# Four sums of weights per unit of a Strassen down projection: two by accumulating transfers from GpSimd's queue, two on VectorE

## The chip, the cores and the metric

The kernel runs on one core of a Trainium2 chip. A core has a matrix engine (TensorE, PE in the profile), a vector engine (VectorE, DVE), a scalar engine (ScalarE, ACT), a general engine (GpSimd, POOL) and a sync engine (SyncE, SP), each with its own instruction queue. Transfers between main memory and the core's on-chip memory are issued from these queues and carried out by 16 DMA engines. The metric is the time of one execution in microseconds, the median of several runs.

## What is computed

The kernel is one inference step of one encoder layer for 1024 prompt frames and 128 sample frames, in float32:

```python
def swiglu(x, w_gate, w_up, w_down):
    return (jax.nn.silu(x @ w_gate) * (x @ w_up)) @ w_down
...
        x = x + 0.5 * swiglu(rms_norm(x, norm_ffn1[l]), w_ffn1_gate[l], w_ffn1_up[l], w_ffn1_down[l])
        m, s_new, conv_new, pool_new = mixer(rms_norm(x, norm_mix[l]), w_in[l], conv_w[l], a_log[l],
        ...
        x = x + m
        x = x + 0.5 * swiglu(rms_norm(x, norm_ffn2[l]), w_ffn2_gate[l], w_ffn2_up[l], w_ffn2_down[l])
```

The model is 1024 wide, the hidden layer of the SwiGLU 2816. The mixer (gated DeltaNet and multi-scale pooling) is not touched here. The change lies in the last product of each SwiGLU, `@ w_down`, which runs twice per execution.

## The kernel before

**Float32 from three products.** A matrix is split into a high part (rounded by a cast) and a low part (what is left), and each product of weights W and operand H is formed as high x high + high x low + low x high. Every block of weights therefore goes through `piece` (L275): ACT casts it into the high half of a tile of the ring O (L287), DVE subtracts to get the low half (L288). PE's matmuls all stand on one line, L58.

**Chunks and units.** The 1152 tokens are three chunks: chunk 0 of 512, chunks 1 and 2 of 320 each. The down projection of chunk 0 (`down0`) is a plain product. Chunks 1 and 2 go together through `down12`, a Strassen-Winograd scheme: the weights are cut into 2 x 2 blocks a11, a12, a21, a22 and seven products of sums of blocks replace eight. One *unit* (g, d) of `down12` makes the seven products for one column block d of the output (d = 0 to 3) and one group g of hidden blocks. The groups have 4, 3 and 4 blocks of 128, so a unit has 84 matmuls in groups 0 and 2 (weight tiles of 128 x 512), and 63 in group 1 (128 x 384). There are 12 units per stage and two stages, 24 units in all.

**The sums.** Three products take a block as it is (a11, a12, a22), four take sums, all formed by POOL before the change:

- T1 takes a21 + a22 (L282),
- T2 takes `sm` = a21 + a22 + a11 (L286, in the same call of `piece`),
- B22 takes `sm` + a12 (L282),
- T3 takes a11 + a21 (L282).

The buffers of the sums are "s" and "sum", two of each, in region Q for groups 0 and 1, and in A5 for group 2.

**Where the blocks come from.** `load` issues two DMAs from SP per unit, one with a11 and a12 (L642), one with a21 and a22 (L643), 512 KB each with four blocks, 384 KB with three. Their targets are a ring of four slots (R0, R1, O5, O6), so that a load waits until the blocks of the unit two before are used up. Right after the second load SP issues up to 10 pending loads of operands of the next group (`pace`, g_keep to the A and B regions).

**Order.** A scheduler fixes each engine's order; on each engine it is followed strictly. PE's order in a steady unit u is B11(u), B21(u), T4(u-1), T2(u), B22(u), T1(u+1), T3(u). T1 and B22 accumulate in PSUM tile c, B11, T2, T3 and T4 in tile a, B21 in tile b; between two accumulations DVE adds the state of the tile into x (`add`, L654), and the next product on that tile waits for it. T1 of the next unit is formed ahead, inside the present unit (`fifth`).

Of the kernel before, what the change touches and what calls it, by code (L numbers as in the profile page):

```python
# [10 lines left out]
ALU = mybir.AluOpType  # L11
AX = mybir.AxisListType

P = 128
# [12 lines left out]
GROUPS = [(0, 4), (4, 3), (7, 4)]  # L27
# [13 lines left out]
def trunk(ctx: ExitStack, tc: tile.TileContext, xin, s0, convst, poolst, cm_in, vec_in, small_in,  # L41
# [3 lines left out]
    V, A, G, T, SY = nc.vector, nc.scalar, nc.gpsimd, nc.tensor, nc.sync  # L45

    class Products:

        t = 0.0
# [22 lines left out]
    def nm(s):  # L72
        uid[0] += 1
        return f"{s}_{uid[0]}"

    def pt(tag, shape=None):
        t = psum.tile([P, 512], F32, tag=tag, name=nm("ps_" + tag))
        return t
# [16 lines left out]
    def region(tag, dt=F32):  # L95
        return main.tile([P, SIZE[tag]], dt, tag=tag, name=nm(tag))
# [17 lines left out]
    def xk(c, k):  # L114
        return X[c][k // 4][:, k % 4, :]

    class Slots:


        def __init__(self):  # L120
            self.mem, self.n = {}, {}
# [28 lines left out]
    def pace(ins, most=1):  # L150

        with tc.issue_after(ins):
            for _ in range(min(most, len(pending))):
                pending.pop(0)()
# [113 lines left out]
    class Blocks:  # L268


        def __init__(self, ring):
            self.gs, self.ring, self.n = Slots(), ring, 0

        def piece(self, *src, more=None):

            m = src[0].shape[-1]
            t = region(self.ring[self.n % len(self.ring)], F32R)
            self.n += 1
            hi, lo = t[:, :m], t[:, 512:512 + m]
            if len(src) == 2:  # L280
                t = self.gs.get("s", m)
                G.tensor_add(t, *src)  # L282
                src = [t]
            src = src[0]
            if more:
                G.tensor_add(more[0], src, more[1])  # L286
            Blocks.high = A.copy(hi, src).ins  # L287
            Blocks.mark = V.tensor_sub(lo, src, hi.bitcast(F32)).ins  # L288
            return [x.rearrange("p (k c) -> p k c", c=P) for x in (hi, lo)]

        def product(self, ps, w, hs, start=True, stop=True):
            (whi, wlo), (hhi, hlo) = w, hs
            for k in range(len(hhi)):
                T.matmul(ps, whi[:, k, :], hhi[k], start=start and k == 0, stop=False, skip_group_check=True)
                T.matmul(ps, whi[:, k, :], hlo[k], start=False, stop=False, skip_group_check=True)
                T.matmul(ps, wlo[:, k, :], hhi[k], start=False, stop=stop and k == len(hhi) - 1, skip_group_check=True)
# [44 lines left out]
    def gate_up(wi, wg, wu, gk, H, RB, cs, ahead, norm, x0=None):  # L341


        bl = Blocks([f"O{i}" for i in range(7)])
        gs, piece, product = bl.gs, bl.piece, bl.product

        def load(f, most=1):
# [55 lines left out]
        def fifth(w):  # L403

            be, sm, c3 = pt("c")[:, :N], gs.get("sum", 512), gs.get("c3", N)
            product(be, piece(w[2], w[3], more=(sm, w[0])), op["T1"])
            A.mul(c3, be, -1.0)
            return c3, sm

        def left_gate(al, g1, g2):  # L410

            p1, ga = gs.get("p1", N), pt("b")[:, :N]
            w1 = piece(g1)
            product(al, w1, op["B11"])
            A.copy(p1, al)
            w2 = piece(g2)
            product(ga, w2, op["B21"])
            V.tensor_add(p1, p1, ga)
            A.activation(p1, p1, AF.Silu)
            return p1, w1, w2  # L420
# [191 lines left out]
    def down12(wd, gk, op0, beside, done):  # L612


        bl = Blocks(["O3", "O4", "O0", "O1", "O2"])
        gs, piece, product = bl.gs, bl.piece, bl.product
        for tag in ("R0", "R1", "O5", "O6"):
            gs.place(region(tag), ("raw", 1024, 1))

        def temps(tag):  # L620
            for t in ("s", "sum"):
                gs.mem.pop(t, None)
            gs.place(region(tag), ("s", 512, 2), ("sum", 512, 2))

        ops = {0: op0}

        def ask(g, tags):

            q, n = GROUPS[g]
            op = ops[g] = {}  # L630
            for j, (name, tag) in enumerate(zip(DOWN, tags)):
                t = region(tag, F32R)
                op[name] = [[t[:, (2 * k + s) * N:(2 * k + s + 1) * N] for k in range(n)] for s in range(2)]
                for k in range(n):
                    pending.append(lambda t=t, j=j, k=k: SY.dma_start(
                        t[:, 2 * k * N:2 * (k + 1) * N].bitcast(F32), gk[2][q - AHEAD // 2 + k][j]))

        def load(g, d, most):
            q, n = GROUPS[g]
            o, m = 2 * q * P, n * P  # L640
            raws = gs.get("raw", 2 * m), gs.get("raw", 2 * m)
            SY.dma_start(raws[0], wd[d][:, o:o + 2 * m])  # L642
            pace(SY.dma_start(raws[1], wd[d + 4][:, o:o + 2 * m]).ins, most)  # L643
            return [r[:, i * m:(i + 1) * m] for r in raws for i in range(2)]

        def fifth(g, d, w):

            be, sm = pt("c")[:, :N], gs.get("sum", w[0].shape[-1])
            product(be, piece(w[2], w[3], more=(sm, w[0])), ops[g]["T1"], True, False)
            add(2, d + 4, be, -0.5)  # L650
            return be, sm

        def add(c, d, ps, by=0.5):
            V.scalar_tensor_tensor(xk(c, d), ps, by, xk(c, d), ALU.mult, ALU.add)  # L654

        def ended(g, c, d):
            if g == len(GROUPS) - 1 and done:
                done(c, d)

        def left_low(g, d, al, a22):  # L660

            product(al, piece(a22), ops[g]["T4"], False)
            add(1, d + 4, al, -0.5)
            ended(g, 1, d + 4)

        temps("Q")
        units = [(g, d) for g in range(len(GROUPS)) for d in range(4)]
        nxt = last = None
        ask(1, ["A5", "A0", "A1", "A2", "A3", "A4", "A6"])
        for u, (g, d) in enumerate(units):  # L670
            if not nxt:
                w = load(g, d, 6)
                nxt = w, fifth(g, d, w)
            (a11, a12, a21, a22), (be, sm) = nxt
            op = ops[g]
            al, ga = pt("a")[:, :N], pt("b")[:, :N]
            product(al, piece(a11), op["B11"])
            add(1, d, al)
            product(ga, piece(a12), op["B21"])
            next(beside, None)  # L680
            if last:
                left_low(*last)
            if u == 4:
                ask(2, [f"B{i}" for i in range(7)])
            product(al, piece(sm), op["T2"], False)
            add(1, d, ga)
            ended(g, 1, d)
            add(2, d, al)
            product(be, piece(sm, a12), op["B22"], False)
            add(2, d, be)  # L690
            ended(g, 2, d)
            next(beside, None)
            if u + 1 < len(units):
                g2, d2 = units[u + 1]
                if g2 == 2 and g == 1:
                    temps("A5")
                w = load(g2, d2, 6 if g2 == 0 else 10)
                if g2 != g:
                    rest()
                nxt = w, fifth(g2, d2, w)  # L700
            product(al, piece(a11, a21), op["T3"], False)
            add(2, d + 4, al, -0.5)
            ended(g, 2, d + 4)
            next(beside, None)
            last = g, d, al, a22
        left_low(*last)
        for _ in beside:
            pass
# [38 lines left out]
    def downs(wd, gk, src, done0=None, after=lambda c: (), done12=None):  # L747
# [33 lines left out]
        down0(wd, [(home, first, 0), (second, ask, 2)], sums(), done0)  # L781
        rest()
        down12(wd, gk, op0, iter(after(0)), done12)

        ends = [iter(after(c)) for c in (2, 1)]
# [23 lines left out]
    def rest():  # L809
        while pending:  # L810
            pending.pop(0)()
# [642 lines left out]
    for n in names:  # L1454
        if n[1] in "dHXr":
            continue
        b, w, h = n[0], n[1], n[2]
# [38 lines left out]
    left = list(urgent)  # L1496
    while left or fill or live or cur:
# [4 lines left out]
        if cur is None and fill and all(i in done for i in after[fill[0]]):  # L1502
            n = fill.pop(0)
            cur = [n, max([done[i] for i in after[n]] + [0]), None]
        cand = sorted([(e[0] > T.t, e[0] if e[0] > T.t else 0, n[0], rank[n[1]], n) for n, e in live.items()])
        if cand and (not cand[0][0] or cur is None or cur[1] > cand[0][1]):
            n = cand[0][-1]
            e = live[n]
        elif cur:
            n, e = cur[0], cur[1:]  # L1510
# [165 lines left out]
```

## Time and profile before

| | |
|---|---|
| median of 3 runs | 2192.55 us (2190.09 to 2193.48) |
| profiled execution | 2195.53 us, span 2193.7 us |
| mean granted clock of PE | 0.992 |
| PE, DVE, ACT, POOL busy | 2132.2, 1526.1, 917.5, 684.9 us |
| moved by DMA | 289.72 MB |
| first stage of `down12` | about 621 to 787 us |
| second stage of `down12` | about 2004 to 2177 us |

The profile is of one execution. "Busy" sums the durations of an engine's instructions. A view of waits lists, by line, how long an engine stood idle and which instruction released it: total, number of times, longest. In a timeline each row has the start, the duration, the engine, line and operation, "out<-in", and in brackets the idle time ahead of it with the releaser. Rows of the chain of waits tell which piece of work the last instruction of a stretch had been waiting for, step by step. A row of the DMA view has the number of transfers, their size and the median time from issue to landing. All times are in us from the start of the span.

### The profile page before, as it was taken

To read this page: it belongs to the slowest core of one execution; us is meant where nothing else is said; L and a number is where in the kernel's file an instruction comes from. 1 tells how busy PE (TensorE), PEld (TensorE's weight loads), DVE (VectorE), ACT (ScalarE), POOL (GpSimd) and SP (SyncE) were. 2 spreads that over 40 slices of the span, in tenths; PEclk is the share of its full clock that TensorE was granted. 3 is DMA by queue.
4 is the path that set the end of the run, shared out by engine and by line. 5 is a ranking of instruction groups with operands and counts; after the bars stand their busy time and mean duration, and the time that the engine had idled before them with its cause. 6 is when DMAs were issued, how large, how long until landed. Compare 5 with 4: busy or idle time off the path is not lost.

```text
span 2193.7 us, 33164 instructions
## 1 busy us (share of the span) xinstructions
PE 2132.2 (97%) x12341; PEld 1920.7 (88%) x12341; DVE 1526.1 (70%) x2736; ACT 917.5 (42%) x1854; POOL 684.9 (31%) x616
## 2 busy tenths in 40 slices
PE   9999999999999999999999998999999999999997
PEld 7899999998889887777989887889999999987997
DVE  7866666677347877778687867776666668743776
ACT  6433333444223455544444443543433335422333
POOL 1433333440014422322232333243333335100443
PEclk9999999999999999999999999999999999999998
DMA  6332333554556522111212123342333337446572
GB/s 252 120 124 103 128 109 112 183 202 147 184 195 218 179 86 61 57 61 59 94 55 80 44 93 93 134 145 92 127 110 123 115 129 248 142 125 225 198 256 74
DMA packets 102674, 289.72 MB, mean 132 GB/s; under 512 B 16240, under 2 KB 24304, under 8 KB 102256
## 3 DMA queue, kind: packets, MB, share of 16 engines
q1 hardware_dynamic: 101360, 286.40, 38.6%
q8 instruction: 97, 1.59, 0.3%
q10 hardware_dynamic: 1152, 1.19, 0.2%
q14 instruction: 65, 0.53, 0.1%
HBM read 214.89 MB, written 72.66 MB: 131 GB/s over the span
## 4 chain that ended last, share of the span: by engine, by line
PE 82%; DVE 10%; issue 2%; DMA 2%; POOL 2%; ACT 2%; DVEq 0%; SPq 0%; POOLq 0%; ACTq 0%
PE ps_a L58 31%; PE ps_b L58 20%; PE ps_d L58 17%; PE ps_c L58 14%; DVE O L288 2%; DVE B L981 1%; DVE O L186 1%; DVE A L1121 1%; PE ps_b L62 1%; DVE A L1323 1%; DMA x<-g_keep 1%; DVE x L654 1%; DMA R<-in_wd 1%; DVE A L1120 0%; POOL Q L282 0%
## 5 line engine op out<-in xcount | busy, mean ns | idle before, releaser
L58 PE MATMUL ps_a<-B,O 128*128 128x320 f32 x3040 | 509.1, 311 | 9.0 <-DVE x L654 5.8
L58 PEld LDWEIGHTS ps_a<-B,O 128*128 128x128 f32 x3040 | 465.7, 189 | 20.5 <-issue 8.6
L58 PE MATMUL ps_a<-A,O 128*128 128x320 f32 (+1 forms) x1952 | 426.3, 354 | 2.9 <-DVE A L1121 1.6
L58 PEld LDWEIGHTS ps_a<-A,O 128*128 128x128 f32 x1952 | 330.0, 190 | 37.6 <-issue 3.9
L288 DVE TENSOR_TENSOR O<-Q,O 128x512 fp32r<-128x512 f32 (+1 forms) x238 | 210.6, 886 | 193.6 <-ACT O L287 192.7
L58 PE MATMUL ps_b<-A,O 128*128 128x512 f32 (+1 forms) x1128 | 264.5, 388 | 5.2 <-ACT O L287 5.2
L58 PEld LDWEIGHTS ps_b<-A,O 128*128 128x128 f32 x1128 | 208.9, 189 | 45.8 <-ACT O L287 5.2
L58 PE MATMUL ps_d<-A,O 128*128 128x512 f32 x1056 | 244.2, 391 | 2.7 <-DVE x L606 1.8
L58 PEld LDWEIGHTS ps_d<-A,O 128*128 128x128 f32 x1056 | 196.8, 188 | 49.0 <-issue 4.0
L287 ACT CAST O<-Q 128x512 fp32r<-128x512 f32 (+1 forms) x238 | 143.2, 605 | 225.2 <-POOL Q L282 60.8
L288 DVE TENSOR_TENSOR O<-R,O 128x512 fp32r<-128x512 f32 (+1 forms) x216 | 197.7, 920 | 33.2 <-ACT O L287 32.4
L58 PE MATMUL ps_d<-B,O 128*128 128x320 f32 (+1 forms) x1104 | 206.1, 331 | 5.4 <-DVE x L1002 3.7
L282 POOL TENSOR_TENSOR Q<-R 128x512 f32<-128x512 f32 (+1 forms) x44 | 59.9, 1361 | 453.7 <-DMA R<-in_wd 279.0
L58 PE MATMUL ps_c<-A,O 128*128 128x512 f32 (+1 forms) x816 | 187.2, 377 | 0.8 <-DVE O L288 0.8
L58 PEld LDWEIGHTS ps_d<-B,O 128*128 128x128 f32 x1104 | 172.2, 189 | 16.1 <-DVE x L1002 5.9
L287 ACT CAST O<-R 128x512 fp32r<-128x512 f32 (+1 forms) x216 | 131.1, 611 | 126.5 <-PE ps_a L58 51.3
L58 PEld LDWEIGHTS ps_c<-A,O 128*128 128x128 f32 x816 | 145.6, 188 | 25.0 <-DVE O L288 1.3
L185 ACT CAST O<-R 128x1024 fp32r<-128x1024 f32 (+1 forms) x86 | 85.9, 1010 | 183.6 <-PE ps_d L58 133.7
L58 PE MATMUL ps_c<-B,O 128*128 128x320 f32 x912 | 144.6, 309 | 0.0
L58 PEld LDWEIGHTS ps_c<-B,O 128*128 128x128 f32 x912 | 136.8, 188 | 0.3
L393 POOL TENSOR_TENSOR A<-A,A 128x512 fp32r<-128x512 f32 x44 | 72.6, 1651 | 162.3 <-ACT A L392 162.2
L186 DVE TENSOR_TENSOR O<-R,O 128x1024 fp32r<-128x1024 f32 (+1 forms) x74 | 86.5, 1176 | 50.6 <-ACT O L185 29.7
(309 smaller groups left out, 3061.4 us busy)
## 6 DMA issues: line engine op xcount, KB each, us to landing
g_keep<-x SPq DMA_DIRECT2D x98, 320.0 KB, 2.5
R<-in_wg SPq DMA_DIRECT2D x48, 512.0 KB, 3.8
R<-in_wd SPq DMA_DIRECT2D x48, 512.0 KB, 3.7
R<-in_wu SPq DMA_DIRECT2D x47, 512.0 KB, 3.6
g_keep<-A SPq DMA_DIRECT2D x44, 512.0 KB, 2.6
A<-g_keep SPq DMA_DIRECT2D x44, 512.0 KB, 5.5
B<-g_keep SPq DMA_DIRECT2D x56, 320.0 KB, 6.3
A<-g_keep SPq DMA_DIRECT2D x42, 320.0 KB, 5.0
```

The source lines that it names most:

```text
L58: self.put(nc.tensor.matmul(out, lhs, rhs, **k), n / 2400 + .003 if lhs.dtype == F32R else max(n, lhs.shape[-1]) / 600)
L62: self.put(nc.tensor.transpose(out, lhs, rhs), out.shape[-1] / 1200)
L185: A.copy(hi, raw)
L186: (e or V).tensor_sub(lo, raw, hi.bitcast(F32))
L282: G.tensor_add(t, *src)
L287: Blocks.high = A.copy(hi, src).ins
L288: Blocks.mark = V.tensor_sub(lo, src, hi.bitcast(F32)).ins
L393: G.tensor_sub(go[:, 1], sg, go[:, 0].bitcast(F32))
L654: V.scalar_tensor_tensor(xk(c, d), ps, by, xk(c, d), ALU.mult, ALU.add)
L981: V.scalar_tensor_tensor(y[:, :512], raw[:, t:t + 512], cw[:, t:t + 1], y[:, :512], ALU.mult, ALU.add)
L1121: V.tensor_tensor(Uc[:, :, m + 1:], Uc[:, :, m + 1:], tu[:, :n, :w], ALU.add)
L1323: V.tensor_tensor(buf[:, :, :have], cur[:, :, w_:w_ + have], cur[:, :, :have], ALU.add)
```

## The change

`Blocks` gets a parameter `e`, the engine of its adds; `down12` passes VectorE, so that `sm` (L286) and the sum for B22 (L282) move to DVE. The gate and up projections keep GpSimd. The two other sums are formed in memory: `summed` issues a plain DMA of one block and then an accumulating DMA of the other into the same buffer, both from GpSimd's queue and straight from main memory; the second waits for the first to have landed. `low` = a21 + a22 is asked for in `load`, `left` = a11 + a21 at the end of the unit before. The sums' region, which held "s" and "sum" twice, now holds "s", "sum", "low" and "left" once each. The loads of the raw blocks stay as they are; a21 is still loaded there, though nothing reads it any more.

```diff
-        def __init__(self, ring):
-            self.gs, self.ring, self.n = Slots(), ring, 0
+        def __init__(self, ring, e=G):
+            self.gs, self.ring, self.n, self.e = Slots(), ring, 0, e
...
             if len(src) == 2:
                 t = self.gs.get("s", m)
-                G.tensor_add(t, *src)
+                self.e.tensor_add(t, *src)
                 src = [t]
             src = src[0]
             if more:
-                G.tensor_add(more[0], src, more[1])
+                self.e.tensor_add(more[0], src, more[1])
...
-        bl = Blocks(["O3", "O4", "O0", "O1", "O2"])
+        bl = Blocks(["O3", "O4", "O0", "O1", "O2"], V)
...
-            for t in ("s", "sum"):
+            for t in ("s", "sum", "low", "left"):
                 gs.mem.pop(t, None)
-            gs.place(region(tag), ("s", 512, 2), ("sum", 512, 2))
+            gs.place(region(tag), ("s", 512, 1), ("sum", 512, 1), ("low", 512, 1), ("left", 512, 1))
...
-            return [r[:, i * m:(i + 1) * m] for r in raws for i in range(2)]
+
+            low = summed("low", m, wd[d + 4][:, o:o + m], wd[d + 4][:, o + m:o + 2 * m])
+            return [r[:, i * m:(i + 1) * m] for r in raws for i in range(2)] + [low]
+
+        def summed(tag, m, one, other):
+            t = gs.get(tag, m)
+            G.dma_start(t, one)
+            G.dma_start(t, other, accum_op=ALU.add)
+            return t
+
+        def left_sum(g, d):
+            q, n = GROUPS[g]
+            o, m = 2 * q * P, n * P
+            return summed("left", m, wd[d + 4][:, o:o + m], wd[d][:, o:o + m])
...
-            product(be, piece(w[2], w[3], more=(sm, w[0])), ops[g]["T1"], True, False)
+            product(be, piece(w[4], more=(sm, w[0])), ops[g]["T1"], True, False)
...
             if not nxt:
                 w = load(g, d, 6)
+                left = left_sum(g, d)
                 nxt = w, fifth(g, d, w)
-            (a11, a12, a21, a22), (be, sm) = nxt
+            (a11, a12, a21, a22, _), (be, sm) = nxt
...
-            product(al, piece(a11, a21), op["T3"], False)
+            product(al, piece(left), op["T3"], False)
+            if u + 1 < len(units):
+                left = left_sum(*units[u + 1])
+
```

In the changed kernel the lines behind the additions have other numbers: `add` is L667, the plain DMA of `summed` L650, the accumulating one L651.

**POOL's order, a unit of four blocks in the first stage.** Q is the region of the sums, R0 to O6 are the raw slots, `in_wd1` is the weight in main memory. Before, one unit's four adds:

```order
L282 TENSOR_TENSOR Q_522_5464<-R1_519_5461 128x512 [waits DMAHW7_49,DVE_49]
L282 TENSOR_TENSOR Q_522_5464<-O5_520_5462,O6_521_5463 128x512 [waits DVE_49]
L286 TENSOR_TENSOR Q_522_5464<-Q_522_5464,R0_518_5460 128x512 [waits DMAHW6_49,Pool_49]
L282 TENSOR_TENSOR Q_522_5464<-Q_522_5464,R0_518_5460 128x512 [waits DVE_49,Pool_49]
L282 TENSOR_TENSOR Q_522_5464<-O6_521_5463 128x512 [waits DMAHW7_49,DVE_49]
```

Now, at the same place:

```order
L650 DMA Q_522_5464<-in_wd1 128x512 [waits DMASW0_49,DVE_49]
L650 DMA Q_522_5464<-in_wd1 128x512 [waits DMASW1_49,DVE_49]
L651 DMA Q_522_5464<-in_wd1 128x512 [waits DMASW2_49]
L651 DMA Q_522_5464<-in_wd1 128x512 [waits DMASW3_49]
```

The adds waited for the raw loads (DMAHW, the queue of SP). The plain DMAs wait for DVE's use of the sum before (`low` behind the split of T1 and the add of `sm`, `left` behind the split of T3), the accumulating ones for the landing of the plain ones (DMASW, GpSimd's own queue). The first and third row are `low` of the unit after the next, the second and fourth `left` of the next unit.

**DVE's order in the same place.** Before, from T1's update of x on (ps_c is tile c, ps_a tile a; a split from Q is that of a sum):

```order
L654 SCALAR_TENSOR_TENSOR x21_488_5205<-ps_c_538_5574,x21_488_5205 128x320 [waits PE_49]
L288 TENSOR_TENSOR O3_546_5659<-Q_522_5464,O3_546_5659 128x512 [waits Activation_49]
L654 SCALAR_TENSOR_TENSOR x21_488_5205<-ps_a_532_5499,x21_488_5205 128x320 [waits PE_49]
L288 TENSOR_TENSOR O4_547_5676<-Q_522_5464,O4_547_5676 128x512 [waits Activation_49]
L654 SCALAR_TENSOR_TENSOR x10_485_5202<-ps_a_541_5610,x10_485_5202 128x320 [waits PE_49]
L288 TENSOR_TENSOR O0_549_5702<-Q_522_5464,O0_549_5702 128x512 [waits Activation_49]
```

Now:

```order
L667 SCALAR_TENSOR_TENSOR x21_488_5205<-ps_c_538_5579,x21_488_5205 128x320 [waits PE_49]
L288 TENSOR_TENSOR O3_546_5664<-Q_522_5464,O3_546_5664 128x512 [waits Activation_49]
L286 TENSOR_TENSOR Q_522_5464<-Q_522_5464,R0_518_5460 128x512 [waits DMAHW6_49,DMASW0_49,DVE_49]
L667 SCALAR_TENSOR_TENSOR x21_488_5205<-ps_a_532_5502,x21_488_5205 128x320 [waits PE_49]
L288 TENSOR_TENSOR O4_547_5681<-Q_522_5464,O4_547_5681 128x512 [waits Activation_49]
L282 TENSOR_TENSOR Q_522_5464<-Q_522_5464,R0_518_5460 128x512 [waits DVE_49]
L667 SCALAR_TENSOR_TENSOR x10_485_5202<-ps_a_541_5615,x10_485_5202 128x320 [waits PE_49]
L288 TENSOR_TENSOR O0_549_5709<-Q_522_5464,O0_549_5709 128x512 [waits Activation_49]
```

Two adds have come in. The first, `sm` of the unit after the next (L286), waits for the landing of `low` (DMASW0); behind it stand T3's update of x (second L667), the split for B22, the second add, B11's update and, last, the split of `low` for T1 (O0).

**PE's order at the change from group 1 to group 2.** A5 is T1's operand of group 1, and becomes the region of the sums for group 2. Now, from T1 of the last unit of group 1 (ps_c from A5) to T1 of the first unit of group 2 (ps_c from B0):

```order
L58 MATMUL ps_c_605_6304<-A5_523_5465,O0_606_6305 128x320 x9
L58 MATMUL ps_a_598_6224<-A4_528_5470,O1_607_6319 128x320 x9
L58 MATMUL ps_a_608_6334<-A0_524_5466,O2_610_6336 128x320 x9
L58 MATMUL ps_b_609_6335<-A1_525_5467,O3_611_6349 128x320 x9
L58 MATMUL ps_a_598_6224<-A6_529_5471,O4_612_6361 128x320 x9
L58 MATMUL ps_a_608_6334<-A2_526_5468,O0_613_6374 128x320 x9
L58 MATMUL ps_c_605_6304<-A3_527_5469,O1_614_6388 128x320 x9
L58 MATMUL ps_c_616_6407<-B0_576_6033,O2_617_6408 128x320 x12
```

Six products of nine matmuls lie between. On POOL's queue the first `low` of group 2 waits for PE here:

```order
L650 DMA Q_522_5464<-in_wd1 128x384 [waits DMASW5_49,DVE_49]
L651 DMA Q_522_5464<-in_wd1 128x384 [waits DMASW6_49]
L650 DMA A5_615_6402<-in_wd1 128x512 [waits DMAHW1_49,DMAHW2_49,DMAHW0_49,PE_49]
L650 DMA A5_615_6402<-in_wd1 128x512
L651 DMA A5_615_6402<-in_wd1 128x512 [waits DMASW0_49]
L651 DMA A5_615_6402<-in_wd1 128x512 [waits DMASW1_49]
```

Before, the matmuls of the first products of group 2 were interleaved with the last ones of group 1 here; now T1 of group 2 stands whole ahead of T3 of group 1's last unit.

## The prediction

> **What bounds the kernel now.** I read the page first: the busy table, the chain of waits, and the group of adds that the change touches.
>
> ```profile
> PE 2132.2 (97%) x12341; PEld 1920.7 (88%) x12341; DVE 1526.1 (70%) x2736; ACT 917.5 (42%) x1854; POOL 684.9 (31%) x616
> PE 82%; DVE 10%; issue 2%; DMA 2%; POOL 2%; ACT 2%; DVEq 0%; SPq 0%; POOLq 0%; ACTq 0%
> L282 POOL TENSOR_TENSOR Q<-R 128x512 f32<-128x512 f32 (+1 forms) x44 | 59.9, 1361 | 453.7 <-DMA R<-in_wd 279.0
> ```
>
> TensorE (PE) is busy 97% of the span and carries 82% of the chain. The matmuls stay as they are, so the change can only give back, or add to, PE's stops inside the two stages of `down12` (about 621 to 787 us and 2004 to 2177 us). The view of PE's waits lists those stops, the first stage first:
>
> ```profile
> PE ps_a L58 <- DVE O L288: 2.2, 1, 2.2
> PE ps_a L58 <- DVE x L654: 1.8, 2, 1.2
> PE ps_a L58 <- ACT O L287: 0.7, 1, 0.7
> PE ps_c L58 <- DVE O L288: 0.4, 1, 0.4
> ...
> PE ps_a L58 <- DVE x L654: 4.9, 6, 2.0
> PE ps_d L58 <- POOL rt L232: 1.7, 2, 1.2
> PE ps_d L58 <- DVE x L606: 1.3, 1, 1.3
> PE ps_c L58 <- DVE O L288: 0.4, 1, 0.4
> ```
>
> L606 and L232 belong to chunk 0 and to the end of the stage. What a unit of `down12` can lose is 2.2 + 1.8 + 0.7 + 0.4 = 5.1 us in the first stage and 4.9 + 0.4 = 5.3 us in the second. After the two longest stops the clock falls too. PE's timeline, a normal stretch first:
>
> ```profile
> 737.17 1.63 PE L58 MATMUL ps_c<-B,O 128*128 128x320 f32 x10
> 744.44 3.04 PE L58 MATMUL ps_a<-B,O 128*128 128x320 f32 x10 [2.17 <-DVE O L288]
> ...
> 2042.07 3.68 PE L58 MATMUL ps_a<-B,O 128*128 128x320 f32 x24
> 2045.59 1.92 PE L58 MATMUL ps_b<-B,O 128*128 128x320 f32 x12
> 2070.52 5.29 PE L58 MATMUL ps_a<-B,O 128*128 128x320 f32 x24 [1.98 <-DVE x L654]
> ```
>
> Ten matmuls after the 2.17 us stop take 3.04 instead of 1.63 us, 24 after the 1.98 us stop 5.29 instead of 3.68: 1.4 and 1.6 us more. All that can be won is 5.1 + 1.4 + 5.3 + 1.6 = 13.4 us.
>
> The same rows give the beat of a unit: 24 matmuls in 2045.59 - 2042.07 = 3.52 us, so a product of 12 is 1.76 us and one of 9 is 1.32; a unit of seven is 12.3 us with four row blocks, 9.24 with three.
>
> What is late at such a stop is told by the chain of waits that ends at 2070.52, here its larger pieces:
>
> ```profile
> 2058.12 4.20 DMA O<-in_wd
> ...
> 2062.45 1.31 POOL Q L282
> ...
> 2063.78 0.63 ACT O L287
> ...
> 2065.88 1.39 DVE O L288
> 2067.27 1.71 DVE x L1579
> ...
> 2070.52 1.62 PE ps_a L58 x9
> ```
>
> A raw half (512 KB) is asked for only when a slot of the ring comes free, lands 4.2 us later, and only then does POOL add a21 + a22 (T1's operand), ACT cast it and VectorE (DVE) split it. DVE waits for this and then has a heap to catch up, at a bad price, since it runs beside POOL's next adds:
>
> ```profile
> 664.63 1.12 DVE L288 TENSOR_TENSOR O<-Q,O 128x512 fp32r<-128x512 f32 x1 [3.14 <-ACT O L287]
> 667.78 1.38 DVE L288 TENSOR_TENSOR O<-R,O 128x512 fp32r<-128x512 f32 x1
> ...
> 2069.30 0.68 DVE L288 TENSOR_TENSOR O<-O,O 128x512 fp32r<-128x512 f32 x1
> 2069.90 0.48 DVE L654 SCALAR_TENSOR_TENSOR x<-ps_a,x 128x320 f32<-128x320 f32 x1
> 2070.30 0.68 DVE L288 TENSOR_TENSOR O<-O,O 128x512 fp32r<-128x512 f32 x1
> ...
> 733.56 0.54 DVE L288 TENSOR_TENSOR O<-O,O 128x384 fp32r<-128x384 f32 x1
> ```
>
> A split is 0.68 us alone (0.54 with three blocks), 1.12 to 1.38 beside POOL.
>
> **The change part by part.** POOL's four adds per unit go: 96 in all, off PE's path except through the chain above. With them goes the heap's cause: a21 + a22 no longer waits for a raw slot. T4 still reads a22 from the raw half, but T4 stands late in a unit, so a late landing has most of a unit to arrive.
>
> DVE gets two adds per unit, 32 of 0.68 and 16 of 0.54 = 30 us in all. They lie beside PE's products; against them stand the splits that no longer run beside POOL, some four per unit at 0.44 us (1.12 - 0.68) or more less. I take DVE as even. If that cover is gone the adds are on the path where DVE's row is full:
>
> ```profile
> 712.00:722.00 10.00, 9.59 (x64) 9.09 (x64) 7.91 (x15) 3.58 (x8) 4.19 (x5) 1.00 1.02 391
> 745.00:758.00 13.00, 13.00 (x83) 13.00 (x82) 11.07 (x24) 5.18 (x10) 3.33 (x3) 0.90 0.35 99
> ...
> 2065.00:2075.00 10.00, 8.02 (x46) 7.79 (x45) 10.00 (x16) 3.52 (x6) 3.35 (x3) 0.84 0.37 108
> 2105.00:2118.00 13.00, 13.00 (x91) 13.00 (x90) 9.43 (x21) 4.22 (x10) 5.50 (x5) 1.00 1.02 385
> ```
>
> (Columns: PE, PEld, DVE, ACT, POOL busy, PE's clock, DMA share, GB/s.) DVE is full only from 2065 to 2075; elsewhere 2 us or more of a unit are free.
>
> POOL's queue gets 96 DMAs, four per unit: `low` plain, `left` plain, `low` accumulating, `left` accumulating. The accumulating one waits until the plain one has landed. So what the change adds is a wait of length **L**, from T1's split of one unit (which frees the only `low` buffer) to the landing of the next `low`: two issues and two landings in a row. No row of this trace shows a DMA from POOL. The nearest rows:
>
> ```profile
> R<-in_wd SPq DMA_DIRECT2D x48, 512.0 KB, 3.7
> B<-g_keep SPq DMA_DIRECT2D x56, 320.0 KB, 6.3
> R<-in_wd SPq DMA_DIRECT2D x24, 384.0 KB, 3.2
> x<-x_keep SPq DMA_DIRECT2D x2, 256.0 KB, 2.8
> ...
> 2043.28 0.33 SPq L643 DMA_DIRECT2D R<-in_wd  x1
> ```
>
> Low end: SP's issue twice and 2.8 twice, 2 x (0.33 + 2.8) = 6.3 us. High end: POOL's mean add as the issue and 5.3 as the landing (midway from 4.2 to the 6.3 of queued transfers), 2 x (1.36 + 5.3) = 13.3. I take an issue of 1.0 (POOL's instructions are slower than SP's), 2.8 for the plain 256 KB and, because an accumulation moves the destination as well, the 3.7 of 512 KB for the second: L = 1.0 + 2.8 + 1.0 + 3.7 = **8.5 us**. With three blocks (192 KB): 1.0 + 2.6 + 1.0 + 3.2 = 7.8.
>
> The Trainium skill, "DMA: Bandwidth & Descriptors", section on the anatomy of a DMA from GpSimd, fits such a DMA at 2.0 us plus the bytes over 436 GB/s, 2.6 us for 256 KB; the pair would be 5.2 us, an estimate from that page, which says nothing there of an accumulation's price. By it all would be hidden; no run here shows it yet.
>
> What L costs. DVE waits for `low` at the head of sm = low + a11 (L286), and behind that stands T3's update of x (L667), which T4 needs before it may write the same PSUM tile. Three prices follow.
>
> *Slack of one wait.* The split of T1(u+1) comes 0.4 + 0.6 = 1.0 us after B11(u). From there to T4(u) PE has eight products, 8 x 1.76 = 14.1. L286 and L667 need 0.6 + 0.48 = 1.1 of it. Slack: 14.1 - 1.0 - 1.1 = 12.0, so L = 8.5 stops nothing. Three blocks: 10.6 - 0.9 - 0.9 = 8.8, against 7.8.
>
> *The loop.* From one landing to the next the DVE does L286, L667, L288, L282, L667, L288, starts 0.6 and 0.4 apart: 3.3 us (2.7 with three blocks). The loop is L + 3.3 against 12.3, so it holds PE back from L = 9.0 on; with three blocks 7.8 + 2.7 = 10.5 against 9.24, 1.3 late per turn. There are two such turns per stage; the first eats the slack of 1.0, the second costs 0.3. Both stages: 0.6 us.
>
> *The change from group 1 to 2.* There `low` moves into A5, which holds T1's operand of group 1 until T1(7) ends. T1(8) stands six products later, 6 x 1.32 = 7.9 us. L + cast 0.63 + 0.4 of the split - 7.9 = 1.6 us. Both stages: 3.2 us.
>
> *Sum.* Of the 13.4 us I leave 3.0 for stops made by DVE's other work (L1579 above, 1.71 us in the chain). -13.4 + 3.0 + 0.6 + 3.2 = **-6.6 us**. The profiled execution took 2195.5 us, 3.0 over the median of 2192.55; it would become 2188.9, the median 2186.
>
> **The rivals.**
>
> *B: nothing to see, about 2191.* With L at 9.4 (8.7 with three blocks) four blocks still live on their slack; group 1 costs 8.7 + 2.7 - 9.24 - 0.1 = 2.1 per stage, the change of group 2.5, both stages 9.2: -10.4 + 9.2 = -1.2. The adds on a full DVE around 2065 (two units, 2 x 1.36 = 2.7 us) lead there as well. So does the change not doing what it says: the halves a11, a12 and a22 are still loaded, and if they were late for B11 or T4 the stops would stay. Against that: the chain names POOL's add.
>
> *C: slower, the pair of transfers sets the beat.* It decides from L = 9.9, where its costs reach 15 us. At L = 10.0: the loop 13.3 against 12.3 over six turns of four blocks, less the slack of 2.0 twice, 2.0; group 1 (9.3) 0.5 + 2.8 = 3.3; the change of group 3.1; both stages 16.8, net +6.4: 2199. At 10.6 the three are 6.8, 4.5 and 3.7, both stages 30, net +19.6: 2212. For it: the windows above show the DMA engines full (1.02, 391 and 385 GB/s) in group 1 of both stages, where the new transfers must share; 320 KB take 6.3 us there. Against it: these are long queues on one ring, and POOL's is another (no row shows how they share).
>
> *D: POOL's issuing is held up by DVE.* If a DMA's issue from POOL had to wait for a running DVE instruction, as POOL's adds and DVE's splits hold each other up (1.38 against 0.68), up to 1.4 us would come on each issue: L = 8.5 + 2.8 = 11.3. Loop 2.3 x 6 - 1.4 = 12.4, group 1 5.9, change of group 4.4, both stages 45: +35, 2227. The Trainium skill has this as a trap, "SBUF — State Buffer", "Who interferes with whom" and its summary of rules (hide no GpSimd DMA under a DVE instruction), but for two-port modes, which it says `tensor_tensor` lacks. By it this rival falls away; no run here shows it.
>
> **How the numbers follow.** The runs of before span 0.15%, so under 0.2% (4.4 us) counts as no change. By the sums above faster needs L below about 8.9, slower L above 9.9. The forecast, faster, 2186 us: 0.45, its own range 2180 to 2188. B 0.22, C 0.27, D 0.06. Faster 0.45, same 0.22, slower 0.33. The range begins at 2179, where all 13.4 us come back and nothing new stops, and ends at 2213, C at 10.6; 0.08 lies below and 0.12 above.
>
> **What would show it.** Right: from a `low` transfer's issue to the accumulated landing 8 to 9 us; PE's stops at L667 gone within units of four blocks, and one of about 1.6 us ahead of T1(8) in each stage; splits at 0.68 us throughout. Wrong: DVE waiting at L286 for `low` in every unit (C), POOL's DMA issues beyond 1.5 us (D), or PE still stopping for a DVE that is busy all the time (B).

## The result: slower by 2.1%

The changed kernel takes 2239.09 us (median; 2237.52 to 2243.74) against 2193.22 us of the kernel before on the same chip: ratio 1.0215, 95% interval 1.0201 to 1.0229, some 46 us more. 2186 us was forecast, with 0.45 for faster, and a range that ended at 2213.

The page of the changed kernel: busy times, the queue that is new, and the chain of waits.

```profile
span 2235.7 us, 33250 instructions
...
PE 2141.0 (96%) x12341; PEld 1931.1 (86%) x12341; DVE 1519.8 (68%) x2784; ACT 918.2 (41%) x1854; POOL 623.7 (28%) x616
...
q0 software_dynamic: 10496, 23.07, 4.9%
...
PE 75%; DMA 10%; DVE 7%; issue 5%; ACT 2%; POOL 1%; DVEq 0%; SPq 0%; POOLq 0%; ACTq 0%
```

The span is 42.0 us longer. PE's busy time is 8.8 us longer with the same matmuls: they run slower after stops (24 of them take 5.32 us after the first stop below, 3.68 elsewhere), and the mean granted clock is 0.985 instead of 0.992. The other 33 us are stops. In the chain DMA has gone from 2% to 10%; the transfers that fill the sums (into Q and A) have 6% and 3% of it. VectorE is *less* busy than before, 1519.8 against 1526.1 us, though it does 48 more adds.

PE's waits in the two stages of `down12`, the first stage first:

```profile
PE ps_c L58 <- ACT O L287: 8.2, 2, 5.6
PE ps_a L58 <- DVE x L667: 7.7, 2, 6.4
PE ps_a L58 <- ACT O L287: 7.0, 2, 4.2
...
PE ps_a L58 <- DVE x L667: 7.9, 5, 2.6
PE ps_a L58 <- ACT O L287: 7.0, 2, 5.7
PE ps_c L58 <- ACT O L287: 6.4, 1, 6.4
PE ps_d L58 <- POOL rt L232: 1.8, 2, 1.2
PE ps_a L58 <- issue: 1.7, 1, 1.7
```

22.9 us and, without L232's, 23.0 us, where there were 5.1 and 5.3. The same stops on PE's timeline of the first stage:

```profile
667.86 5.32 PE L58 MATMUL ps_a<-B,O 128*128 128x320 f32 x24 [6.39 <-DVE x L667]
719.21 4.36 PE L58 MATMUL ps_a<-A,O 128*128 128x320 f32 x18 [4.23 <-ACT O L287]
736.71 2.83 PE L58 MATMUL ps_c<-A,O 128*128 128x320 f32 x9 [2.58 <-ACT O L287]
740.83 5.14 PE L58 MATMUL ps_a<-A,O 128*128 128x320 f32 x18 [1.30 <-DVE x L667]
757.09 3.76 PE L58 MATMUL ps_c<-B,O 128*128 128x320 f32 x12 [5.60 <-ACT O L287]
781.84 3.75 PE L58 MATMUL ps_a<-B,O 128*128 128x320 f32 x24 [2.75 <-ACT O L287]
```

The first lies in the first units, the next three in group 1, the fifth is T1 of group 2, the last in group 2. Behind them stand the pairs of transfers. From the chain of waits (plain transfer, then the accumulating one), for the pairs of `low` ahead of the first, second, fifth and sixth stop, and last one from group 0 of the second stage:

```profile
651.33 6.83 DMA Q<-in_wd
...
658.45 8.09 DMA Q<-in_wd
...
705.56 5.57 DMA Q<-in_wd
...
711.42 6.65 DMA Q<-in_wd
...
742.97 6.52 DMA A<-in_wd
...
749.79 6.61 DMA A<-in_wd
...
771.77 2.84 DMA A<-in_wd
...
774.89 5.67 DMA A<-in_wd
...
2071.18 3.00 DMA Q<-in_wd
...
2074.47 7.09 DMA Q<-in_wd
```

From the first issue to the last landing that is 15.2, 12.5, 13.4 and 8.8 us, and 10.4 us in the second stage, where the pairs before and after it take 10.7 and 11.0. In the prediction the pair, L, had 7.8 us in group 1 and 8.5 elsewhere. Issuing is not what makes it long; it is over within the first microsecond of each transfer and is part of these times (771.77 and 774.89 stand in both views). POOL's timeline, the first row the start of the pair ahead of the third stop:

```profile
721.34 0.58 POOL L650 DMA_DIRECT2D Q<-in_wd  x1 [7.51 <-DVE O L288]
...
771.77 0.57 POOL L650 DMA_DIRECT2D A<-in_wd  x1 [7.25 <-DVE O L288]
...
774.89 0.89 POOL L651 DMA_DIRECT2D A<-in_wd  x1 [1.56 <-DMA A<-in_wd]
```

The wait that the prediction described, DVE held at `sm` (L286) with T3's update (L667) behind it, is there. DVE's timeline at the second and the sixth stop:

```profile
718.15 0.56 DVE L286 TENSOR_TENSOR Q<-Q,R 128x384 f32<-128x384 f32 x1 [5.99 <-DMA Q<-in_wd]
718.63 0.48 DVE L667 SCALAR_TENSOR_TENSOR x<-ps_a,x 128x320 f32<-128x320 f32 x1
...
780.65 0.69 DVE L286 TENSOR_TENSOR A<-A,R 128x512 f32<-128x512 f32 x1 [3.09 <-issue]
781.25 0.48 DVE L667 SCALAR_TENSOR_TENSOR x<-ps_a,x 128x320 f32<-128x320 f32 x1
```

`low` had landed at 718.07 and 780.56, just ahead of the adds. The updates end at 719.11 and 781.73, and PE goes on at 719.21 and 781.84. The view of PE's waits puts these two stops down to a cast of ACT, but that cast had ended some 0.5 us before. In 11 of the 24 units DVE waits in this way, 2.8 to 9.1 us each.

Casts wait for the sums as well. ScalarE's timeline in group 1, where a cast from Q is that of a sum:

```profile
718.17 0.51 ACT L287 CAST O<-Q 128x384 fp32r<-128x384 f32 x1 [5.28 <-DMA Q<-in_wd]
720.01 0.51 ACT L287 CAST O<-Q 128x384 fp32r<-128x384 f32 x1 [1.33 <-DMA Q<-in_wd]
721.99 0.51 ACT L287 CAST O<-R 128x384 fp32r<-128x384 f32 x1 [1.47 <-PE ps_a L58]
...
736.14 0.51 ACT L287 CAST O<-Q 128x384 fp32r<-128x384 f32 x1 [8.06 <-DMA Q<-in_wd]
```

The first is the cast of `low` for T1, the second that of `left` for T3, the third that of a raw block, which stands behind both in ACT's queue and then waits for PE. The last is the cast of the next `low`, whose pair began at 721.34: 14.8 us before.

### The profile page after: what moved, and what is told of

Same layout as the page of the kernel before. It is cut to its first block, busy times and chain, and to the rows that moved or that the text cites. A ratio compares the mean times of both kernels' runs of the same rounds, so it can differ in the third digit from the quotient of the medians.

```text
span 2235.7 us, 33250 instructions
## 1 busy us (share of the span) xinstructions
PE 2141.0 (96%) x12341; PEld 1931.1 (86%) x12341; DVE 1519.8 (68%) x2784; ACT 918.2 (41%) x1854; POOL 623.7 (28%) x616
## 4 chain that ended last, share of the span: by engine, by line
PE 75%; DMA 10%; DVE 7%; issue 5%; ACT 2%; POOL 1%; DVEq 0%; SPq 0%; POOLq 0%; ACTq 0%
PE ps_a L58 27%; PE ps_b L58 18%; PE ps_d L58 17%; PE ps_c L58 13%; DMA Q<-in_wd 6%; DMA A<-in_wd 3%; DVE B L998 1%; DVE A L1138 1%; PE ps_b L62 1%; DVE A L1340 1%; DVE O L186 1%; DMA x<-g_keep 1%; DVE A L1137 1%; DVE B L1141 0%; DMA g_keep<-x 0%
## 5 line engine op out<-in xcount | busy, mean ns | idle before, releaser
L58 PE MATMUL ps_a<-A,O 128*128 128x320 f32 (+1 forms) x1952 | 431.1, 358 | 14.5 <-ACT O L287 9.9
L58 PEld LDWEIGHTS ps_a<-A,O 128*128 128x128 f32 x1952 | 335.6, 193 | 49.2 <-ACT O L287 13.5
L288 DVE TENSOR_TENSOR O<-Q,O 128x512 fp32r<-128x512 f32 (+1 forms) x240 | 197.6, 825 | 177.3 <-ACT O L287 176.5
L58 PEld LDWEIGHTS ps_c<-B,O 128*128 128x128 f32 x912 | 139.7, 191 | 13.9 <-ACT O L287 12.5
L650 POOL DMA_DIRECT2D Q<-in_wd x32 | 18.5, 577 | 355.6 <-ACT O L185 217.5
```

The source lines that it names most:

```text
L58: self.put(nc.tensor.matmul(out, lhs, rhs, **k), n / 2400 + .003 if lhs.dtype == F32R else max(n, lhs.shape[-1]) / 600)
L650: G.dma_start(t, one)
```

## The experiments

Ratios are to the kernel before, with the 95% interval, each against runs on the same chip.

| kernel | ratio | interval |
|---|---|---|
| the change | 1.0215 | 1.0201 to 1.0229 |
| second transfer plain | 1.0117 | 1.0100 to 1.0135 |
| only `left` by transfers | 1.0080 | 1.0058 to 1.0102 |
| only `low` by transfers | 1.0119 | 1.0098 to 1.0140 |
| all four sums on VectorE | 0.9930 | 0.9915 to 0.9946 |
| a21 not loaded | 1.0208 | 1.0186 to 1.0230 |
| the same, two buffers for `low` and `left` | 1.0037 | 1.0025 to 1.0050 |
| all on VectorE, transfers that nobody reads | 0.9949 | 0.9934 to 0.9964 |
| all on VectorE, gate and up too | 0.9907 | 0.9884 to 0.9930 |
| half prefetch | 1.0185 | 1.0168 to 1.0202 |
| only `left`, two buffers | 0.9973 | 0.9961 to 0.9985 |
| two sums on VectorE, two on GpSimd | 0.9975 | 0.9965 to 0.9984 |
| thin prefetch | 1.0137 | 1.0119 to 1.0156 |

### All four sums on VectorE

`Blocks(..., V)` in `down12` stays, `low` and `left` go:

```diff
-            product(be, piece(w[4], more=(sm, w[0])), ops[g]["T1"], True, False)
+            product(be, piece(w[2], w[3], more=(sm, w[0])), ops[g]["T1"], True, False)
...
-            product(al, piece(left), op["T3"], False)
+            product(al, piece(a11, a21), op["T3"], False)
```

> All four sums on VectorE from the raw halves, no transfer from GpSimd's queue, buffers as before the change. Theory (VectorE's adds are cheap since nothing runs beside them on GpSimd): within 6 us of the kernel before, 2187 to 2199. Rival (VectorE's adds are what costs): four adds instead of two per unit, above 2250.

Measured 0.9930: not within 6 us, but 15 us *faster* than before, so that VectorE's adds cost nothing that shows (its busy time grows by 21 us, 1547.4 against 1526.1), and the 13.4 us of the prediction could be had by them alone. PE's waits in the first and second stage, those of `down12` (the page's first line, and DVE's longest wait at an add, from the first stage):

```profile
PE 2122.3 (98%) x12341; PEld 1914.8 (88%) x12341; DVE 1547.4 (71%) x2832; ACT 917.3 (42%) x1853; POOL 550.5 (25%) x520
...
PE ps_a L58 <- ACT O L287: 0.5, 1, 0.5
...
PE ps_a L58 <- DVE x L665: 0.3, 2, 0.2
...
DVE Q L282 <- DMA R<-in_wd: 3.4, 1, 3.4
```

10.4 us of stops have become 0.8. The raw halves are still late now and then (3.4 us at one add), and PE doesn't stop for it. What has changed beside them is seen in the splits from Q in the first stage; before, and in this run:

```profile
L288 DVE TENSOR_TENSOR O<-Q,O 128x512 fp32r<-128x512 f32 (+1 forms) x31 | 26.2, 844 | 17.5 <-ACT O L287 17.0
```

```profile
L288 DVE TENSOR_TENSOR O<-Q,O 128x512 fp32r<-128x512 f32 (+1 forms) x31 | 19.2, 623 | 2.0 <-ACT O L287 1.4
```

The same 31 splits take 623 ns instead of 844 once POOL adds nothing beside them, and the wait for their casts has gone from 17.0 to 1.4 us. The adds are shorter too: 0.62 to 0.68 us on average by kind on VectorE, 1.2 to 1.7 us on GpSimd before.

### Two sums on VectorE, two on GpSimd

Half of the change alone, `sm` and the sum for B22:

```diff
-                self.e.tensor_add(t, *src)
+                (e or self.e).tensor_add(t, *src)
...
+            product(be, piece(w[2], w[3], more=(sm, w[0]), e=G), ops[g]["T1"], True, False)
...
+            product(al, piece(a11, a21, e=G), op["T3"], False)
```

> One half of the change alone: the sums for T2 and B22 on VectorE, those for T1 and T3 on GpSimd as before, no transfers. If the stops of the kernel before come from the raw half being late for a21 + a22, as the prediction has it, they stay: ratio 0.999 to 1.002. If they come from GpSimd's adds themselves (1.29 to 1.75 us each and the splits beside them at twice their time), about half of the gain of all sums on VectorE: ratio 0.995 to 0.998.

0.9975: a gain, about a third of that of all four. PE's stops in the two stages fall from 10.4 to 5.8 us. So part of the stops came from two of POOL's adds and what they do to DVE. The rest stays with the other two; a21 + a22, still POOL's, waits for the raw half as before, so this run alone doesn't say how much of the rest is the late half.

### One sum by transfers

Only `left` (`low` on VectorE), and only `low` (`left` on VectorE):

> `low` is formed by VectorE from the raw halves (three adds per unit on VectorE), only `left` comes by two transfers. Theory: with `low`'s wait gone the time is back near the kernel before, 2185 to 2197, because `left` is wanted six products later than `low`. Rival (VectorE's adds are what costs): worse than the changed kernel, above 2245. Rival (crowding by the extra transfers delays the raw loads): half of the bytes, so half of the loss, about 2215.

> `left` is formed by VectorE from the raw halves, only `low` comes by two transfers. Theory: `low`'s wait stays, 2228 to 2240; a little better than the changed kernel, since `left`'s issues no longer stand between `low`'s two. Rival (crowding): half of the loss, about 2215. Rival (VectorE's adds): above 2245.

Against all sums on VectorE, `left` alone costs 1.5% of the time (33 us) and `low` alone 1.9% (41 us); both together 2.9% (62 us). The theory that I had for these runs is half wrong: `left` was expected to be free, and it costs more than the theory allowed (2207 us). The time of `low` alone, 2215 us, is below the 2228 of the theory and near what the rival, crowding, had given; these two runs don't exclude it. In the run with `left` alone ScalarE waits for it in group 1:

```profile
717.00 0.92 ACT L287 CAST O<-Q 128x384 fp32r<-128x384 f32 x2 [9.08 <-DMA Q<-in_wd]
...
730.00 0.51 ACT L287 CAST O<-Q 128x384 fp32r<-128x384 f32 x1 [5.79 <-DMA Q<-in_wd]
730.42 0.92 ACT L287 CAST O<-O 128x384 fp32r<-128x384 f32 x2
```

and PE stops for the casts behind it (4.1 us just after the first). T3 comes late, but its cast stands early in ACT's queue.

### Two buffers for `left`

```diff
-            gs.place(region(tag), ("s", 512, 2), ("sum", 512, 1), ("left", 512, 1))
+            gs.place(region(tag), ("s", 512, 1), ("sum", 512, 1), ("left", 512, 2))
```

> As the run with only `left` by transfers (ratio 1.008), but `left` has two buffers (the sums for T1 and B22 share one instead of two), so that each pair can be issued a unit earlier. Theory (`left` is waited for where its cast stands in ScalarE's queue, six products ahead of T3, and one buffer leaves it less than a unit): the loss goes, ratio 0.993 to 0.999. Rival (the traffic or the pair as such): ratio stays at 1.006 to 1.010.

From 1.0080 to 0.9973, as the theory has it. The pairs and their bytes are the same; each can be issued a unit earlier. So for `left` it is the single buffer that costs, and not the traffic. This run also bears on the kernel before: in its first stage DVE waits 10.6 us for raw halves, and PE stops 0.8 us.

### a21 not loaded, and two buffers for both sums

The block that nothing reads is not loaded, and (second kernel) its room goes to second buffers:

```diff
-            raws = gs.get("raw", 2 * m), gs.get("raw", 2 * m)
+            raw, a22 = gs.get("raw", 2 * m), gs.get("a22", m)
...
-            gs.place(region(tag), ("s", 512, 1), ("sum", 512, 1), ("low", 512, 1), ("left", 512, 1))
+            gs.place(region(tag), ("s", 512, 1), ("sum", 512, 1), (a, 512, 2))
+            gs.mem[b] = list(spare)
```

> The changed kernel without the load of a21, which nothing reads there: each second raw load is 256 KB (192 KB) instead of 512 KB (384 KB), a quarter of the extra traffic less; buffers of the sums and order stay. Theory (one buffer per sum, so the next pair of transfers starts only when the split before is done; crowding only lengthens the pair in group 1 and at the stage's start): a few microseconds back, 2222 to 2236 on the scale on which the changed kernel has 2239. Rival (traffic itself delays the raw loads): a quarter of the loss or more, below 2222.

> As the run without a21, and the freed memory gives `low` and `left` two buffers each (the second pair of buffers in O6; for group 2 `low` has those in O6, so that it need not wait for A5). Same traffic as the run without a21. Theory (the wait is a loop through the single buffer): with a whole unit more for each pair the stops go, and the time falls to that with all four sums on VectorE or a little above, ratio to before 0.993 to 1.000. Rival (crowding, or the transfers as such): as the run without a21, ratio 1.012 or more.

Less traffic alone does nothing that can be told (1.0208, where a few microseconds were expected); two buffers bring 1.7%, to 1.0037, though not to the 1.000 that I gave as the upper end. PE still stops 11.7 us in the first stage, most of it from 727 to 752, at the end of group 1 and the change to group 2 (here `left` is the one that moves into A5). A plain transfer there:

```profile
729.08 1.38 POOL L655 DMA_DIRECT2D A<-in_wd  x2
738.37 0.89 POOL L656 DMA_DIRECT2D A<-in_wd  x1 [7.90 <-DMA A<-in_wd]
```

It is over 9 us from its issue to the accumulating one that waits for it.

### The second transfer plain

```diff
-            G.dma_start(t, other, accum_op=ALU.add)
+            G.dma_start(t, other)
```

> The second transfer of each sum is a plain one instead of an accumulating one: the same bytes from memory, the same waits, the same order, but the addition is left out (the sums then hold one block only). Theory (the pair of transfers of `low`, L, sets the beat; the accumulation alone takes 5.7 us where the engines are quiet, the plain one 2.8): L falls by about 3 us to 6 us in quiet stretches and stays above 10 where the DMA engines are full, so some 15 to 25 us come back: 2215 to 2225. If only the accumulation is dear and crowding is not: all of the 46 us and more, 2185 to 2195. If the transfers are not the cause but the adds on VectorE: no change, 2239.

1.0117: some 21 of the 46 us come back, as expected for a pair that is long for two reasons. Accumulating as such has a part in it, and is not the whole: the pairs stay long, 13.8 us instead of 15.2 at the first units, 11.9 instead of 12.5 and 10.9 instead of 13.4 ahead of the second and fifth stop, 8.9 where it was 8.8 ahead of the sixth. What accumulating costs alone is seen in the changed kernel at the last pair of the second stage, where no other transfer is under way (2199.97 to 2207.5). Single transfers in the DMA view of short windows, the plain one and the accumulating one behind it:

```profile
A<-in_wd POOLq DMA_DIRECT2D x1, 256.0 KB, 2.9
...
A<-in_wd POOLq DMA_DIRECT2D x1, 256.0 KB, 4.3
```

The pair takes 7.5 us there. In the run with `low` alone an accumulating transfer of the same size takes 6.7 us beside two raw loads.

### Less prefetch beside the pairs

Two kernels with the change, one with half of each prefetched operand of group 2, one with one block of each operand of groups 1 and 2:

```diff
+                    w = N if g == 2 else 2 * N
...
-                        t[:, 2 * k * N:2 * (k + 1) * N].bitcast(F32), gk[2][q - AHEAD // 2 + k][j]))
+                        t[:, 2 * k * N:2 * k * N + w].bitcast(F32), gk[2][q - AHEAD // 2 + k][j][:, :w]))
```

```diff
-                for k in range(n):
+                for k in range(1):
```

> The changed kernel, but the operands of group 2 are prefetched by half only (the high parts; the low parts are left out, and the products take the high part twice), so that 4.5 MB less per stage are moved during group 1. Nothing else is moved. Theory (the pair is long because it shares the engines with that prefetch, 12 to 17 us instead of 9): the stops in group 1 and at the change to group 2 shrink, 15 to 25 us come back, ratio to before 1.010 to 1.015. Rival (the pair is as long by itself): ratio stays at 1.021.

> The changed kernel, but of the operands of groups 1 and 2 only the first block of each is prefetched (7 transfers instead of 21 and 28; the other blocks' products take the first block instead, so the output is another). GpSimd's queue, the sums and their waits stay. The half prefetch kept the number of packets and left the engines 88 to 95% busy in group 1, so it told little. Theory (the pairs are long because they share the engines with the prefetch): the stops at the first units, in group 1 and part of those at the change to group 2 go, the pair falls to 8 to 10 us everywhere: ratio to before 0.997 to 1.009. Rival (the pair is too long by itself, prefetch or not): ratio 1.015 or more.

The half prefetch missed (1.0185) and was a weak test: rows half as long in as many packets. DMA's share from 715 to 725 us, in the change, with the half and with the thin prefetch (columns as in the prediction's windows):

```profile
715.00:725.00 10.00, 5.79 (x29) 5.82 (x30) 5.89 (x13) 2.12 (x5) 1.15 (x2) 0.83 1.06 360
```

```profile
715.00:725.00 10.00, 7.73 (x44) 7.50 (x43) 6.48 (x14) 2.56 (x5) 1.15 (x2) 0.83 0.88 264
```

```profile
715.00:725.00 10.00, 9.59 (x54) 9.43 (x54) 7.08 (x15) 3.08 (x6) 2.94 (x4) 0.83 0.49 120
```

The thin prefetch does empty the engines, and brings 0.8% (17 us): between the two theories. The crowding by prefetch is a part, some 17 of the 46 us; the rest stays without it. The pairs did not fall to 8 to 10 us everywhere: they take 12.0 us at the first units and 11.3 and 7.7 in group 1. The pair at the change to group 2 is as long as ever:

```profile
733.12 6.19 DMA A<-in_wd
...
739.60 7.23 DMA A<-in_wd
```

At that point three sums and two raw loads are on their way at once.

### Traffic alone

```diff
+            summed("spare", m, wd[d + 4][:, o:o + m], wd[d + 4][:, o + m:o + 2 * m])
```

> All four sums on VectorE, and beside it GpSimd's queue does the 24 pairs of `low` (plain, then accumulating) into a buffer that nothing reads, one after the other without pause. It prices the traffic alone. Theory (the waits cost, not the traffic): within 5 us of the run with all sums on VectorE, ratio to before 0.992 to 0.997; the pair takes about 9 us where the engines are quiet and 12 or more in group 1. Rival (crowding of the raw loads): half of what the change costs against all sums on VectorE, ratio above 1.005.

0.9949 against 0.9930; the intervals overlap. It is a weak test of crowding, though: without a reader the pairs run as soon as the queue lets them, in the first stage eight of twelve before `down12` begins, and the other four from 729 us on. What it shows is that pairs that nobody waits for cost next to nothing there; in group 1 it tells nothing.

### A better kernel

> All four sums on VectorE as before, and the sums of the gate and up projections (44 and more adds on GpSimd) on VectorE too. A look for a better kernel: if the splits beside GpSimd's adds are what holds PE there as well, a few microseconds less than the run with the sums of `down12` alone on VectorE, ratio to before 0.989 to 0.993; if VectorE is full in those stages, more, above 0.995.

With the sums of the gate and up projections on VectorE too (`bl = Blocks([...], V)` in `gate_up`): 0.9907, 2170.43 us, the lowest of all runs and below both kernels. From the kernel with the four sums of `down12` on VectorE (0.9930) it can't be told apart: the intervals overlap.

## Why the prediction was wrong

**What bounds the kernel** was right in size: 13.4 us was to be won, and all sums on VectorE win 15. The cause that it named isn't borne out. It had the raw half come late for a21 + a22, and took the slow splits for what follows from it. With the adds off POOL the raw halves are still late (3.4 us, and 10.6 us in the run with two buffers for `left`), and PE's stops are nearly gone all the same (0.8 us in both stages, and 0.8 us in the first). So it takes POOL's adds to make the stops. Whether their length or the slowed splits beside them matter more, and what the late half adds to them, no run takes apart.

**The adds on DVE** "as even": right, even better than that (DVE 6.3 us less busy than before). That DVE was full only from 2065 to 2075 was misread: in the kernel before it was busy 12.86 of 13.00 us from 732 to 745, too.

**The size of L** is the step that failed. The prediction used one L for all places, 8.5 us (7.8 with three blocks). Where nothing competes the pair takes 7.5 us, less than that: the accumulating landing was taken too short (3.7; 4.3 measured), but the issues were added to landings that contain them (1.0 each; 0.57 and 0.89 measured). Where the DMA engines are busy it takes far more: 15.2 us at the first units (DMA share 1.02 from 651 to 667), 12.5 and 14.8 in group 1, 13.4 at the change of group, and 10.4 to 11.0 in group 0 of the second stage (share 0.85 to 0.92 beside these three). The windows quoted in the prediction said that the DMA engines are full in group 1, and the row of 6.3 us for 320 KB said what this does to a transfer; I put them into rival C as something "for it", and the sum took 7.8 us for precisely that place. Its own high end for L was 13.3 us, but its range ended with 10.6.

**What L costs.** By PE's timelines the stops of both stages are 12.9 us in group 0, 15.0 in group 1, 12.0 at the change of group and 5.8 in group 2, where the prediction had 0, 0.6, 3.2 and 0, and 3.0 us of old stops left over. The kinds of wait are the predicted ones, but not all of the prices hold with the measured L:

- *Slack.* In group 1 it holds: 12.5 - 8.8 = 3.7 us, measured 4.23. The 12.0 us of slack with four blocks don't hold. Ahead of the first stop PE had work for 10.1 us from the pair's issue on, ahead of the sixth, where the pair before had landed late, for 7.3 us; less 1.1 us for L286 and L667 the slack is 9.0 and 6.2: 15.2 - 9.0 = 6.2 and 8.8 - 6.2 = 2.6, measured 6.39 and 2.75.
- *The loop* holds. In group 0 of the second stage three pairs of 10.4 to 11.0 us are 13.9, 14.7 and 14.4 us apart, where PE's beat is 12.3, and PE stops 1.63, 2.25 and 2.62 us. For group 1 the sum was short by itself: two turns of 1.3 us less a slack of 1.0 make 1.6 us, not 0.3.
- *The change of group.* 13.4 + 1.0 - 7.9 = 6.5 us lies near the 5.60 measured, but partly by luck. The first `low` in A5 stands in GpSimd's queue behind a pair in Q whose accumulating half waits for its plain one, and is issued only 3.4 us after T1(7) ends; against that PE, slowed and stopped, takes 12 us for the six products instead of 7.9. In the second stage L is 9.5 us there, the wait in the queue 5.6, and the stop 6.42.

So rival C was the right one; with 0.27 it had too little, and its upper end of 10.6 us for L was passed in most of the crowded places.

**`left` at nothing** is the second failed step. It got no price, and no reason was given for it. T3 comes late, but its cast doesn't: it stands in ACT's queue ahead of the next unit's casts, and with one buffer `left` can be issued only when the split before is done. Alone it costs 33 us against VectorE; the changed kernel with `left` formed by VectorE is 21 us faster (1.0119 instead of 1.0215).

**Rival D**, POOL's issue held up by DVE, is excluded: in both stages a plain issue takes 0.56 to 0.63 us and an accumulating one 0.85 to 0.91, beside a DVE that is busy 68% of the span and whose splits and adds are `tensor_tensor`. That agrees with the Trainium skill, "SBUF — State Buffer", "Who interferes with whom". **The Trainium skill's price** of 5.2 us for the pair (an estimate from "DMA: Bandwidth & Descriptors", by its fit of 2.6 us a transfer) is near the plain transfer alone (2.9) and fits no pair of 256 KB in this kernel (7.5 us where nothing competes).

**What stays open.** With two buffers for both sums 1.07% is left against all sums on VectorE; its stops lie around the change of groups, where several pairs and loads meet, but no run took these apart. How the 46 us divide among accumulation, crowding and the single buffer isn't additive: plain transfers bring back 1.0%, a thin prefetch 0.8%, two buffers 1.7%. And no run moved L286 back in DVE's order: it forms `sm` of the unit after the next, and T3's update needn't wait for it.

## What to carry to other kernels

A transfer that a single buffer ties to the consumer before it has a deadline, and is priced at the load of the DMA engines in that place, read from the window in which it will run, not from the median of a quiet row. Its deadline is where the first instruction that reads it stands in an in-order queue, here a cast, and not where the product comes. And before an add is turned into transfers it pays to try it on the engine that has room: VectorE did all four sums, and the splits beside them got faster.

## What the runs showed of the hardware

- An accumulating transfer of 128 x 512 float32 from GpSimd's queue lands 4.3 us after its issue where nothing competes, a plain one 2.9; GpSimd is busy for 0.89 and 0.57 us. Beside one or two raw loads of 512 KB the accumulating one takes 5.7 to 6.7. With the prefetch in full flow a pair of 192 KB transfers takes 12.5 to 14.8 us, and one of 256 KB took 15.2.
- Halving the bytes of a transfer without halving its packets frees the DMA engines little: the share fell from 1.06 to 0.88 while the rate fell from 360 to 264 GB/s.
- VectorE with 48 more adds was busy for less time than before (1519.8 against 1526.1 us): its splits from the sums, no longer beside adds on GpSimd, took 619 ns on average in the first stage instead of 844.
